# High-part products first and low-part products last in every token-major weight tile of a hybrid decoder block

## The chip, the cores and the metric

The kernel runs on one core of a Trainium2 chip. The metric is the time of one execution on the device in microseconds (us). Its engines are named as the profile names them: PE (TensorE, matrix products), PEld (loading of PE's stationary operand), DVE (VectorE), ACT (ScalarE), POOL (GpSimd) and SP (SyncE, which issues nearly all transfers here).

## The reference

One decoder block on a sequence of 256 tokens, model width 2048, all in float32. A conditioning vector `c` gives a shift, a scale and a gate for each of two halves of the block.

```python
mod = jax.nn.silu(c) @ w_ada[l] + b_ada[l]
sh1, sc1, g1, sh2, sc2, g2 = jnp.split(mod, 6, axis=-1)

h = modulate(rms_norm(x, norm1_g[l]), sh1, sc1)
proj = h @ w_in[l]                                   # 2048 -> 6144: q, k, v, gb, gc, xt
...
attn = moba_attention(q, k, v)...                    # 8 heads of 128; one causal block at 256 tokens
conv = gb * causal_dwconv(gc * xt, conv_w[l], conv_b[l])
mixed = jnp.concatenate([rms_norm(attn, attn_out_g[l]), rms_norm(conv, conv_out_g[l])], axis=-1)
x = x + g1[:, None, :] * (mixed @ w_out[l])          # 2048 -> 2048

h2 = modulate(rms_norm(x, norm2_g[l]), sh2, sc2)
u = causal_dwconv(h2 @ w_ffn_up[l], ffn_conv_w[l], ffn_conv_b[l])    # 2048 -> 11264
u_gate, u_up = jnp.split(u, 2, axis=-1)
ffn = (jax.nn.silu(u_gate) * u_up) @ w_ffn_down[l]   # 5632 -> 2048
x = x + g2[:, None, :] * ffn
```

## The kernel before

**Two parts of every operand.** PE multiplies in a reduced form of float32. To keep accuracy, each operand is split: `hi` is the value rounded to that form, `lo` the remainder. A weight tile W and an activation chunk h then give h_hi W_hi + h_hi W_lo + h_lo W_hi, three products in place of one. In `mm_tok`, `a` is the high part of an activation chunk and `b` its low part; both are stationary operands of 128 x 128 (128 input channels by 128 tokens). The weights are the moving operand, 512 columns wide. The result has the tokens on its partitions ("token-major"), and since there are 256 tokens, each 512 columns of output take two PSUM banks, one for each half of the tokens (index `t`).

**Slots.** The work is a list of slots, one for each weight tile of up to 4 x 128 input channels by 512 columns: 48 for the input projection, 16 for the output projection, 176 for the up projection and 52 for the down projection. The input, output and down projections call `mm_tok`. The up projection has its own loop (L705 and L708), with the weights as the stationary operand, in which the products with `hi` weights and those with `lo` weights already stand in separate runs of 16, in either order by turns. In the first 12 slots of the input projection one slot holds two chunks for each of two projections (for instance v0 and v1), and `mm_tok` runs once for each of them, 12 products each. All other tiles of four chunks are one call of 24 products; some tiles of the down projection have three chunks (18 products) or two (12).

**What a tile passes through.** SP issues the load into a `raw` buffer (5 buffers); ACT copies it to `hi` (L235, 3 buffers); DVE subtracts to get `lo` (L241, 3 buffers) and so frees `raw` for the next load; PE reads `hi` and `lo`. Each engine works through its instructions in the order in which they were emitted. A tile's split is emitted two slots ahead, so its `hi` takes the buffer of the slot before the current one and waits until PE has read that one for the last time.

**What stands around it.** The products with `w_ada` run beside all this, partly on PE (L292), partly on DVE (L296 and L298), from the same `raw` buffers. `evac_in` copies (ACT, L412) or adds (DVE, L414) a finished pair of banks to SBUF; a new output takes two of eight banks in turn. `h_chunks` makes the normalized input chunk by chunk when its shift and scale are known (ACT L762 and L766 for the high part, DVE L769 for the low part). `conv_q` sums squares on DVE (L912), and PE finishes that sum (L916, into `ssC`). `norm2` makes the second norm's factors (L569). In the down projection the stationary chunks come from `up_gate` (high part ACT L641, low part DVE L642). A planner fixed the slot of each of these tasks, and their order within a slot, in the table `CFG`.

**Variants of the order.** In `mm_tok`, `order` runs over chunks `k` and token halves `t`. With `by_t`, the first half's products all come before the second's, so that its bank can be emptied earlier (the last tile of the output projection and the last of each column block of the down projection). With `halved`, the very last tile also splits the second half's 512 columns in two.

Of the kernel before, what the change touches and what calls it, by code (L numbers as in the profile page):

```python
# [110 lines left out]
def tile_block(  # L111
# [6 lines left out]
    mm = nc.tensor.matmul  # L118
# [8 lines left out]
    def bank(name):  # L127
        return ps.tile([P, 512], F32, tag="b", bufs=8, name=name)
# [261 lines left out]
    def mm_tok(key, hi, lo, kts, nk, first, last, by_t=False, halved=False):  # L390

        if first:
            mainp[key] = [bank(f"m{key}{t}") for t in range(2)]
        whole = slice(0, 512)
        order = [(k, t, whole) for t in range(2) for k in range(nk)] if by_t else [(k, t, whole) for k in range(nk) for t in range(2)]
        if halved:
            order = order[:nk] + [(k, 1, slice(h, h + 256)) for h in (0, 256) for k in range(nk)]
        for k, t, s in order:
            o = mainp[key][t][:, s]
            a, b = (v[:, t * P:(t + 1) * P] for v in kts[k])  # L400
            mm(o, a, hi[:, k, s], start=(first and k == 0), stop=False)  # L401
            mm(o, a, lo[:, k, s], start=False, stop=False)  # L402
            mm(o, b, hi[:, k, s], start=False, stop=(last and k == nk - 1 and s.stop == 512))  # L403

    def evac_in(f):
        if in_last.get(f) == now[0]:
# [31 lines left out]
    for i, (fs, k) in enumerate(turns):  # L438
        def near(f, d):
            u = uses[f]  # L440
            n = u.index(i) + d
            return 0 <= n < len(u) and abs(u[n] - i) <= 2

        def go(hi, lo, fs=fs, k=k, new=[not near(f, -1) for f in fs], end=[not near(f, 1) for f in fs]):
            m = 4 // len(fs)
            for h, f in enumerate(fs):
                mm_tok(f, hi[:, h::len(fs)], lo[:, h::len(fs)], [halves(hT[k + j]) for j in range(m)], m, new[h], end[h])

        slots.append((pair_load(k, fs[0]) if len(fs) == 2 else w_load(w_in, k, 4, [(COL[fs[0]] * 512, 512)]), 4, go))
        for f in fs:  # L450
            if not near(f, 1):
                at(len(slots), evac_in, f)
            if i == uses[f][-1]:
                in_last[f] = len(slots)
# [78 lines left out]
    for n, (f, part, k) in enumerate(seq):  # L533
        def go(hi, lo, part=part, f=f, k=k, tf=n == len(seq) - 1):
            mm_tok((part, f), hi, lo, [halves(mixT[k + j]) for j in range(4)], 4, k % 8 == 0, k % 8 == 4, tf)
            if k % 8 == 4:
                done.add((part, f))

        slots.append((w_load(w_out, k, 4, [(f * 512, 512)]), 4, go))
        i = len(slots)  # L540
        if f < 3 and k == 4:
            at(i + CFG["hold"][f], hold_a, f)
        elif f < 3 and k == 12:
            at(i + CFG["evac"][f], evac_out, f)
            at(i + CFG["sq"][f], sq_out, f)
            at(i + CFG["tr"][f], tr_out, f)
        elif f == 3 and k == 4:
            at(i, evac_a, f)
            at(i + CFG["part"], ss_part)
# [124 lines left out]
    SEGS, a = [], 0  # L674
# [5 lines left out]
    for seg, (ga, gb_) in enumerate(SEGS):  # L680
# [43 lines left out]
        for f in range(0, 4, 2):  # L724
            k = ka
# [3 lines left out]
        for f, k, n in parts:  # L729
            def go(hi, lo, seg=seg, f=f, k=k, n=n, ka=ka, kb=kb):  # L730
                last = k + n == kb
                mm_tok(("D", seg, f), hi, lo, [gT[k + j] for j in range(n)], n, k == ka, last,
                       last and seg == len(SEGS) - 1, last and seg == len(SEGS) - 1 and f == 3)

            slots.append((w_load(w_down, k, n, [(f * 512, 512)]), n, go))
            if k + n == kb:
                at(len(slots), evac_down, seg, f)
# [41 lines left out]
    for i, (g, r) in enumerate(fill):  # L779
        if i >= n0 + n1 + n2:  # L780
            extra.setdefault(N_OUT + (i - n0 - n1 - n2) // 2, []).append((g, r))
        if r == g.tiles - 1:
            a = N_OUT + 1 + max(0, (i - n0 - n1 - n2) // 2)
# [212 lines left out]
    for half in range(2):  # L996
        xl, gl = max(in_last[f"x{half}"], in_last[f"c{half}"]), in_last[f"g{half}"]
        o = CFG["conv"][half]
# [101 lines left out]
    for i in range(len(slots)):  # L1100
# [16 lines left out]
        hi, lo = splits.pop(0)  # L1117
# [36 lines left out]
```

## Time and profile before

| | |
|---|---|
| median of 3 runs | 1190.57 us (1190.48 to 1191.34) |
| profiled execution | 1190.94 us, of which the span from the first to the last instruction is 1189.2 us |
| mean granted clock of PE | 0.998 |
| DVE busy | 918.7 us, 77% of the span |
| ACT busy | 615.4 us, 52% |
| loaded from HBM | 310.67 MB, 263 GB/s over the span |
| products at L401, L402 and L403 | 866 each |

The profile records one execution. A row of the order of time gives the start (us from the span's start), the length, engine, line, operation, output and inputs, their shapes, and the count of merged instructions; in brackets stands how long the engine had been idle before it, and what released it. A row of waits gives the waiting instruction, what it waited for, the us in total, how often, and the longest. A row of a stretch gives its bounds, its length, then busy us and instructions of PE, PEld, DVE, ACT and POOL, the granted clock, the DMA engines' busy share and GB/s. Products overlap in the records: a product of 512 columns is shown as 0.39 us, while the next one starts 0.23 us after it.

### The profile page before, as it was taken

Reading aid. Unit: us, or ns where it says so; the run is one execution under the profiler, and the core shown is the slowest. Engines: PE = TensorE matmul, PEld = TensorE weight load, DVE = VectorE, ACT = ScalarE, POOL = GpSimd, SP = SyncE. Lnnn points to the kernel's source line nnn. Section 1 sums busy time; section 2 is a strip of 40 time slices with the busy share of each in tenths; the row PEclk is TensorE's granted clock in tenths of the full one; section 3 lists DMA queues with packets and bytes.
Section 4 is the critical chain, followed back from the end, with each engine's and each line's share of the span. In section 5 each row is a group of like instructions: output and inputs, shape, how many; then the busy total and the mean of one; then the engine's idle time right before and its main releaser. Section 6 shows DMA issues by size and latency. Waiting matters only on the chain.

```text
span 1189.2 us, 15487 instructions
## 1 busy us (share of the span) xinstructions
PE 1162.7 (98%) x6047; PEld 964.5 (81%) x6047; DVE 918.7 (77%) x1106; ACT 615.4 (52%) x854; POOL 1.7 (0%) x9
## 2 busy tenths in 40 slices
PE   5999999999999998999999999999999999999998
PEld 3777788877778777888888888888888888888887
DVE  3889989997889998779888579866755667567676
ACT  5554256456765455556654344654544455344452
POOL 0000000000000000000000000000000000000000
PEclk9999999999999999999999999999999999999999
DMA  9999998999769998664776779754475554664533
GB/s 364 376 400 377 375 372 282 367 353 350 274 232 407 356 370 305 212 211 144 248 283 228 264 273 387 252 190 165 168 233 177 192 190 151 215 227 160 192 127 107
DMA packets 195069, 313.78 MB, mean 264 GB/s; under 512 B 6666, under 2 KB 105772, under 8 KB 194740
## 3 DMA queue, kind: packets, MB, share of 16 engines
q1 hardware_dynamic: 194820, 312.73, 73.6%
q8 instruction: 47, 0.77, 0.3%
q14 instruction: 26, 0.21, 0.1%
q10 hardware_dynamic: 176, 0.07, 0.0%
HBM read 310.67 MB, written 2.10 MB: 263 GB/s over the span
## 4 chain that ended last, share of the span: by engine, by line
PE 90%; DVE 4%; DMA 2%; ACT 2%; issue 1%; SPq 1%; DVEq 0%; ACTq 0%
PE z L705 27%; PE z L708 14%; DMA raw<-in_w_ada_dram 2%; PE ada L292 2%; DVE lo L241 2%; PE mx L401 1%; PE mv L403 1%; PE mx L403 1%; PE mx L402 1%; PE mv L401 1%; PE mv L402 1%; PE mc L401 1%; PE mg L401 1%; PE mc L402 1%; PE mc L403 1%
## 5 line engine op out<-in xcount | busy, mean ns | idle before, releaser
L241 DVE TENSOR_TENSOR lo<-raw,hi 128x2048 fp32r<-128x2048 f32 (+2 forms) x204 | 447.6, 2204 | 146.4 <-ACT hi L235 144.7
L235 ACT ACTIVATE hi<-raw 128x2048 fp32r<-128x2048 f32 (+2 forms) x204 | 375.5, 1849 | 326.4 <-PE z L705 74.4
L705 PE MATMUL z<-h,hi 128*128 128x512 f32 x1408 | 329.2, 390 | 1.9 <-DVE h L594 1.1
L705 PEld LDWEIGHTS z<-h,hi 128*128 128x128 f32 x1408 | 261.3, 188 | 55.6 <-DVE h L594 2.0
L708 PEld LDWEIGHTS z<-h,lo 128*128 128x128 f32 x1408 | 174.9, 192 | 3.4
L708 PE MATMUL z<-h,lo 128*128 128x256 f32 x1408 | 176.3, 283 | 0.0
L298 DVE SCALAR_TENSOR_TENSOR ada<-raw,csil,ada 128x1024 f32<-128x1024 f32 (+2 forms) x165 | 159.5, 968 | 5.5 <-DMA raw<-in_w_ada_dram 1.4
L611 DVE TENSOR_TENSOR ub<-z,ub 128x256 f32<-128x256 f32 x104 | 36.8, 417 | 45.7 <-ACT ub L608 45.6
L625 ACT ACTIVATE uy<-ub,fc,fc 128x256 f32<-128x256 f32 x88 | 45.7, 593 | 5.5 <-DVE uy L632 5.5
L292 PE MATMUL ada<-raw,crep 128*32 128x512 f32 (+1 forms) x320 | 36.4, 567 | 9.9 <-DMA raw<-in_w_ada_dram 9.8
L641 ACT ACTIVATE gh<-uy 128x512 fp32r<-128x512 f32 x22 | 13.9, 632 | 61.2 <-DVE uy L639 61.2
L632 DVE SCALAR_TENSOR_TENSOR uy<-ub,fc,uy 128x254 f32<-128x254 f32 x88 | 42.5, 483 | 3.1
L630 DVE SCALAR_TENSOR_TENSOR uy<-ub,fc,uy 128x255 f32<-128x255 f32 x88 | 42.1, 478 | 1.5 <-ACT uy L625 1.5
L608 ACT ACTIVATE ub<-z 128x256 f32<-128x256 f32 x104 | 31.0, 383 | 22.3 <-PE z L705 22.3
L635 ACT ACTIVATE uy<-uy 128x512 f32<-128x512 f32 x22 | 13.9, 631 | 42.1 <-DVE uy L632 42.1
L292 PEld LDWEIGHTS ada<-raw,crep 128*32 128x32 f32 x320 | 8.5, 114 | 25.9 <-issue 14.5
L642 DVE TENSOR_TENSOR gl<-uy,gh 128x512 fp32r<-128x512 f32 x22 | 15.2, 692 | 15.4 <-ACT gh L641 15.4
L401 PE MATMUL mc<-hi,h 128*128 128x512 f32 x64 | 26.2, 409 | 0.0
L401 PE MATMUL mk<-hi,h 128*128 128x512 f32 x64 | 25.3, 396 | 0.7 <-ACT h L766 0.7
L403 PE MATMUL mv<-hi,h 128*128 128x512 f32 x64 | 25.0, 391 | 0.8 <-DVE h L769 0.8
L401 PE MATMUL mq<-hi,h 128*128 128x512 f32 x64 | 25.4, 397 | 0.4 <-DVE pa_q L414 0.4
L401 PE MATMUL mx<-hi,h 128*128 128x512 f32 x64 | 25.5, 399 | 0.0
(548 smaller groups left out, 1861.4 us busy)
## 6 DMA issues: line engine op xcount, KB each, us to landing
raw<-in_w_ada_dram SPq DMA_DIRECT2D x96, 1024.0 KB
raw<-in_w_ffn_up_dram SPq DMA_DIRECT2D x176, 512.0 KB
raw<-in_w_in_dram SPq DMA_DIRECT2D x48, 1024.0 KB
raw<-in_w_ffn_down_dram SPq DMA_DIRECT2D x24, 1024.0 KB
raw<-in_w_ffn_down_dram SPq DMA_DIRECT2D x24, 768.0 KB
raw<-in_w_out_dram SPq DMA_DIRECT2D x16, 1024.0 KB
xr<-in_x_dram SPq DMA_DIRECT2D x2, 1024.0 KB
x<-in_x_dram SPq DMA_DIRECT2D x8, 256.0 KB
```

Of the source, the lines that this page charges most:

```text
L235: act(hi[:, :nk], t[:, :nk], AF.Copy)
L241: V.tensor_tensor(out=lo[:, :nk], in0=t[:, :nk], in1=hi[:, :nk].bitcast(F32), op=ALU.subtract)
L292: mm(self.acc[q:q + 32, :], crep[:, i, :], t[:, j, :], start=(r == 0 and j < 4), stop=(r == self.tiles - 1 and j >= self.rows - 4), tile_p ...
L298: V.scalar_tensor_tensor(out=self.acc, in0=t[:, j, :], scalar=csil[:, i:i + 1], in1=self.acc, op0=ALU.mult, op1=ALU.add)
L401: mm(o, a, hi[:, k, s], start=(first and k == 0), stop=False)
L403: mm(o, b, hi[:, k, s], start=False, stop=(last and k == nk - 1 and s.stop == 512))
L611: V.tensor_tensor(out=d, in0=zp[grp][ft][:, :256], in1=d, op=ALU.add)
L625: act(y, b, AF.Identity, bias=fcols[3][:, i:i + 1], scale=fcols[2][:, i:i + 1])
L630: V.scalar_tensor_tensor(out=y[:, 1:], in0=b[:, :255], scalar=fcols[1][:, i:i + 1], in1=y[:, 1:], op0=ALU.mult, op1=ALU.add)
L632: V.scalar_tensor_tensor(out=y[:, 2:], in0=b[:, :254], scalar=fcols[0][:, i:i + 1], in1=y[:, 2:], op0=ALU.mult, op1=ALU.add)
L705: mm(zp[grp][ft], hi[:, j, ft * P:(ft + 1) * P], h2T[k + j], start=begins and j == 0, stop=ends and j == 3)
L708: mm(zp[grp][ft][:, :256], lo[:, j, ft * P:(ft + 1) * P], h2T[k + j][:, :256], start=False, stop=False)
```

## The change

Within each call of `mm_tok` the triple a·hi, a·lo, b·hi of one chunk and token half is taken apart. All a·hi and b·hi products come first, in the old order of chunks and halves, and all a·lo products follow in the same order. Where a tile goes token half by token half (`by_t`), or column half by column half (`halved`), this holds within each of these parts, since the sort keeps them apart. The flag that starts an accumulation stays on the first a·hi of a bank; the one that ends it moves to the last a·lo. The number of products, their shapes and their operands are the same, and nothing outside `mm_tok` is touched.

```diff
         if halved:
             order = order[:nk] + [(k, 1, slice(h, h + 256)) for h in (0, 256) for k in range(nk)]
-        for k, t, s in order:
+
+        for low, k, t, s in sorted(((low, *e) for low in (False, True) for e in order),
+                                   key=lambda e: (by_t * e[2], e[3].start * halved * e[2], e[0])):
             o = mainp[key][t][:, s]
             a, b = (v[:, t * P:(t + 1) * P] for v in kts[k])
-            mm(o, a, hi[:, k, s], start=(first and k == 0), stop=False)
-            mm(o, a, lo[:, k, s], start=False, stop=False)
-            mm(o, b, hi[:, k, s], start=False, stop=(last and k == nk - 1 and s.stop == 512))
+            if low:
+                mm(o, a, lo[:, k, s], start=False, stop=(last and k == nk - 1 and s.stop == 512))
+            else:
+                mm(o, a, hi[:, k, s], start=(first and k == 0), stop=False)
+                mm(o, b, hi[:, k, s], start=False, stop=False)
```

## The prediction

> **What bounds the kernel now.** I read the page first (engines, then the chain that ended last), then the waits of the matmul engine, then stretches of the order of time. The engines and the head of the chain:
>
> ```profile
> PE 1162.7 (98%) x6047; PEld 964.5 (81%) x6047; DVE 918.7 (77%) x1106; ACT 615.4 (52%) x854; POOL 1.7 (0%) x9
> ...
> PE 90%; DVE 4%; DMA 2%; ACT 2%; issue 1%; SPq 1%; DVEq 0%; ACTq 0%
> ```
>
> PE is busy for 1162.7 of 1189.2 us and carries 90% of the chain. A change of order that leaves the 6047 products alone can win only from the other 26.5 us, and the list of what PE waited for says where part of those are (us in total, times, longest):
>
> ```profile
> PE ada L292 <- DMA raw<-in_w_ada_dram: 9.8, 3, 6.9
> PE n2b L569 <- DVE n2d L567: 1.5, 1, 1.5
> ...
> PE mv L403 <- DVE h L769: 0.8, 1, 0.8
> PE ssC L916 <- DVE sq L912: 0.7, 1, 0.7
> PE mq L401 <- DVE pa_q L414: 0.4, 1, 0.4
> ```
>
> The reader is to see what is not there: PE never waits for lo L241 or hi L235, the two halves of a weight tile. The obvious gift of the change, more time until the low part is needed, pays nothing, because nobody waits for it. The 9.8 us are loads at the start; n2b and two waits after it, left out here, belong to the norm between output projection and up projection. Three waits (mv, ssC, mq) lie in or beside token-major tiles. Whether those move is the whole question.
>
> **Part 1: the products.** Lines 401 to 403 issue 2598 products (a third on each line), and the change keeps them all, with one weight load each (both counts on the page are 6047). What it alters is which follows which. Neighbouring steps of one tile, its first products and its last, the 24th:
>
> ```profile
> 438.37 0.39 PE L401 MATMUL m('C', 3)0_3728<-hi,mix 128*128 128x512 f32 x1
> 438.60 0.39 PE L402 MATMUL m('C', 3)0_3728<-lo,mix 128*128 128x512 f32 x1
> 438.82 0.39 PE L403 MATMUL m('C', 3)0_3728<-hi,mix 128*128 128x512 f32 x1
> ...
> 443.58 0.39 PE L403 MATMUL m('C', 3)1_3729<-hi,mix 128*128 128x512 f32 x1
> ```
>
> 23 steps in 443.58 - 438.37 = 5.21 us make 0.2265 us a product. From L401 to L402 the stationary operand a stays and the moving one changes; from L402 to L403 the stationary changes: 0.23 and 0.22, so the step does not see it. The chain in order of time has the other pattern, one moving operand under several stationary ones, which the change will use:
>
> ```profile
> 495.00 7.28 PE z L705 x32
> ```
>
> 7.28 / 32 = 0.2275 us. Cost of the new order on PE itself: 0. The two patterns differ by 1 ns a step, and I bound the cost by that either way, 2598 x 0.001 = 2.6 us, a case of its own among the rivals; I take 0 because the first pattern (neighbours with and without a shared operand in one tile) shows none.
>
> A rule speaks against the change here. The Trainium skill, "TensorE: Matmul & The Clock Gate", section "Step-by-step: what each phase is for", says that a stationary operand is loaded apart from the product so that one load can serve many products; the change pulls apart the two that share a. By that rule 866 pairs would lose a saved load each. The trace disagrees that anything is saved: each product has its own load and the step is the same with and without a new operand.
>
> **Part 2: the high part is released earlier.** In a tile of four chunks the last read of hi moves from product 24 to 16, that is 8 x 0.2265 = 1.81 us earlier; with three chunks from 18 to 12 (1.36 us); in the tiles that hold two projections, where each runs its own 12 products, from 24 to 20 (0.91 us). lo's last read moves from 23 to 24, 0.23 us later. The up projection already has tiles in which the high products run first, and shows that the buffer is freed in mid-tile:
>
> ```profile
> 916.01 7.44 PE L705 MATMUL z<-h,hi 128*128 128x512 f32 x32
> 923.29 4.00 PE L708 MATMUL z<-h,lo 128*128 128x256 f32 x32
> ...
> 923.49 1.92 ACT L235 ACTIVATE hi<-raw 128x2048 fp32r<-128x2048 f32 x1 [1.36 <-PE z L705]
> ```
>
> The high products end at 916.01 + 7.44 = 923.45, ACT takes the buffer at 923.49, while the low products go on. So wherever ACT waits for a token-major tile, its hi copy, and behind it in DVE's queue the subtraction for lo, the raw buffer's release and SP's next load, can run up to 1.81 us earlier. All of it is off PE's path, except through what stands behind lo in DVE's queue.
>
> **Part 3: what comes free of this, wait by wait.** First mq, where a new tile's second bank waits until the tile before it is copied out:
>
> ```profile
> 171.27 1.92 ACT L235 ACTIVATE hi<-raw 128x2048 fp32r<-128x2048 f32 x1 [2.41 <-issue]
> 174.24 0.16 DVE L345 TENSOR_TENSOR B<-adaz,vbc 128x4 f32<-128x4 f32 x1 [1.54 <-ACT ada L339]
> ...
> 188.03 1.92 ACT L235 ACTIVATE hi<-raw 128x2048 fp32r<-128x2048 f32 x1 [2.67 <-PE mk L403]
> ...
> 198.48 0.39 PE L403 MATMUL mq<-hi,h 128*128 128x512 f32 x1
> 199.58 0.40 PE L403 MATMUL mq<-hi,h 128*128 128x512 f32 x1
> 200.37 0.51 PE L401 MATMUL mq<-hi,h 128*128 128x512 f32 x1 [0.39 <-DVE pa_q L414]
> ...
> 199.63 1.28 DVE L414 TENSOR_TENSOR pa_q<-mq,pa_q 128x512 f32<-128x512 f32 x2
> ```
>
> The old tile's last product ends at 198.48 + 0.39 = 198.87, but DVE is behind and copies only at 199.63; PE's step is 0.79 where 0.23 is due: 0.56 us lost. DVE has stood without a gap since the h chunks behind 174.24, where it waited 1.54 for ACT, and ACT's hi at 171.27 had waited for the tile that ended then; freed 1.81 us earlier, ACT and DVE run up to 1.5 us ahead, and the next hi (188.03, waiting for mk L403) is freed earlier too. Then DVE copies at about 198.9, one bank takes 0.64, and the bank is needed at 199.58 (third product now, not fourth): under 0.1 us is left. I take -0.5. Ends: -0.56, and +0.23 if DVE is no earlier, since the bank is wanted one product sooner.
>
> Second ssC, the sum of squares of the convolution half:
>
> ```profile
> 346.18 1.91 ACT L235 ACTIVATE hi<-raw 128x2048 fp32r<-128x2048 f32 x1 [0.81 <-PE m('A', 0)1_2919 L403]
> 348.13 2.29 DVE L241 TENSOR_TENSOR lo<-raw,hi 128x2048 fp32r<-128x2048 f32 x1 [1.35 <-ACT hi L235]
> 351.56 0.48 DVE L971 SCALAR_TENSOR_TENSOR cv<-cp,v1c,cv 128x255 f32<-128x255 f32 x1 [0.47 <-ACT cv L970]
> ...
> 378.63 1.80 DVE L912 TENSOR_TENSOR sq<-sq 128x256 f32<-128x256 f32 x4
> ...
> 380.57 0.58 PE L916 MATMUL ssC<-ones,sq 128*128 128x1 f32 x4 [0.70 <-DVE sq L912]
> ```
>
> DVE works from 351.56 (where it had waited for ACT, whose work there stands right behind this hi) to 378.63 + 1.80 = 380.43 with no gap, so its lateness goes back to the hi at 346.18, which waited 0.81 us for a tile's end. Freed 1.81 us earlier, that hi gains the 0.81 that ACT stood idle, and DVE's queue with it, if the loads that it uses on the way are there. 0.81 is more than PE's 0.70: I take -0.7; ends -0.7 and 0.
>
> **Part 4: what is needed earlier.** The product with an activation chunk's low part b moves forward too: for chunk j (from 0) of the first bank from product 6j+3 to 4j+2. Where chunks are made just in time, that costs:
>
> ```profile
> 66.32 0.50 PE L401 MATMUL mv<-hi,h 128*128 128x512 f32 x1
> 66.66 0.40 PE L402 MATMUL mv<-lo,h 128*128 128x512 f32 x1
> 67.90 0.50 PE L403 MATMUL mv<-hi,h 128*128 128x512 f32 x1 [0.84 <-DVE h L769]
> ...
> 67.42 0.75 DVE L769 TENSOR_TENSOR h<-hf,h 128x256 fp32r<-128x256 f32 x2
> ```
>
> Here PE does two products and then waits for the chunk. Now only one stands ahead of the wait, so one more is left behind it: +0.23 us. The chunk itself comes no earlier: the chain before it starts from transposes that PE does at the end of an earlier tile.
>
> At the very first tile the same happens and is free:
>
> ```profile
> 25.55 0.42 DVE L769 TENSOR_TENSOR h<-hf,h 128x256 fp32r<-128x256 f32 x1 [1.18 <-ACT h L766]
> 25.57 0.50 PE L401 MATMUL mk<-hi,h 128*128 128x512 f32 x1 [0.72 <-ACT h L766]
> 33.56 1.54 PE L292 MATMUL ada<-raw,crep 128*32 128x256 f32 x16 [2.22 <-DMA raw<-in_w_ada_dram]
> ```
>
> b is ready at 25.97, wanted at about 25.8: 0.2 us, hidden by the 2.22 us in which PE then waits for a load; without that cover +0.2. In the down projection one chunk is close:
>
> ```profile
> 847.08 1.49 ACT L235 ACTIVATE hi<-raw 128x1536 fp32r<-128x1536 f32 x1 [1.27 <-PE m('D', 1, 0)1_7102 L403]
> 851.73 0.69 DVE L642 TENSOR_TENSOR gl<-uy,gh 128x512 fp32r<-128x512 f32 x1 [0.76 <-ACT gh L641]
> 852.77 0.39 PE L403 MATMUL m('D', 1, 0)0_7101<-hi,gl 128*128 128x512 f32 x1
> ```
>
> gl is ready at 851.73 + 0.69 = 852.42 and used at 852.77, the tile's ninth product; it becomes the sixth, 852.09: 0.33 us too late. But the hi ahead of it in the queues waited 1.27 us for a tile of three chunks, which releases 1.36 us earlier, so gl comes about 1 us earlier as well: 0, and +0.33 if not. Last, the first bank of a tile is complete at product 23 instead of 21, 0.45 us later; the second, which ends the copying, at 24 as before: 0. The last tiles of both projections run bank by bank and keep their end.
>
> **Sum.** +0.23 - 0.5 - 0.7 = -0.97, about -1.0 us: span 1188.2, and the profiled execution (1190.94, its span plus 1.7) 1189.9. That execution lay 0.37 over the median of the three runs, 1190.57; the median becomes 1189.6. Ends: -0.56 - 0.70 = -1.3, or +0.23 + 0.23 + 0.33 + 0.2 = +1.0. About 0.2%, 2.4 us, is what a measurement of this kernel can tell from no change; no end reaches it.
>
> **Rivals.** (1) The gain does not come, the earlier needs stay: slower. Loads are near their limit in the stretch that ends at mq:
>
> ```profile
> 120.00:200.00 80.00, 79.97 (x369) 64.08 (x367) 73.45 (x78) 39.08 (x71) 0.00 (x0) 1.00 0.91 343
> ```
>
> The column before the last is the DMA share, 0.91. If DVE is held by the raw tiles' landing rather than by hi, it runs no earlier, and the price is +0.23 at mv, +0.23 at mq and up to +0.33 at gl and 0.2 at the start: 1191.0 to 1191.6. It decides once DVE gains less than 0.2 us before 199 us. Against it: the waits named at 171.27, 188.03 and 346.18 are on PE or unnamed, not on DMA.
>
> (2) PE's step does depend on the operands' order. Each nanosecond a product is 2.6 us. Upward it takes back the forecast's gain from 0.4 ns and gets past 2.4 us from 1.3 ns; at 2 ns, 5.2 us, the time is 1194.8. Downward, 1 ns gives 1187.0. Against it stand the rows of part 1; for it, that no tile yet has the exact sequence "same bank, same moving, new stationary". The skill's rule above would act through this one.
>
> (3) The slow stretch of PE's clock moves.
>
> ```profile
> 35.03 0.80 PE L401 MATMUL mc<-hi,h 128*128 128x512 f32 x1
> 37.61 0.39 PE L401 MATMUL mc<-hi,h 128*128 128x512 f32 x1
> ```
>
> Six products take 2.58 us where 1.36 is due: 1.2 us lost after the wait at 33.56. If a slightly later end of the first tile spares it, the time is 1188.4; if a second stretch follows, up to 1191.3. The Trainium skill, the same page, Part 1, "What's actually happening", has a gate that halves the clock after an idle window of about 3.4 us; the rows agree with half speed.
>
> **How the numbers follow.** Forecast 0.55 (its own range 1189.2 to 1190.2); rival 1 0.25; rival 2 0.10 (0.06 slower, 0.04 faster); rival 3 0.10, of which 0.02 gets past the 2.4 us. So faster 0.06, slower 0.06, within 0.88. The range takes in the forecast, rival 1 and half of rival 3, 1188.7 to 1191.6, and leaves out about 0.15.
>
> **What would show it.** Right: L401 and L403 of a tile come first with L402 last, steps still 0.2265; ACT's hi released by L403 some 1.8 us before a tile's end; no wait at ssC, under 0.1 us at mq; at mv a wait ahead of the second product, about 0.2 us longer. Wrong: steps off by a nanosecond or more, waits of PE on lo, or new waits of PE for chunks or banks above 1 us in total.

## The result, and the profile after

The changed kernel takes 1189.12 us (median of 17 runs, 1188.79 to 1190.10) where the kernel before takes 1191.23 us (median of 17 runs, 1190.01 to 1193.31): ratio 0.9983, 95% interval 0.9976 to 0.9990, that is 1.2 to 2.9 us less. The time lies in the stated range, 0.5 us under the forecast of 1189.6 and just under the forecast's own range (1189.2 to 1190.2). Against the kernel before on the same chip the gain is 2.1 us, about twice the 1.0 us of the forecast's sum and more than its better end of 1.3. The profiled execution took 1190.10 us with a span of 1188.3 and is the slowest of the 17, so the two profiles differ by only 0.84 us.

The page's rows for the engines and the head of the chain:

```profile
PE 1162.6 (98%) x6047; PEld 964.9 (81%) x6047; DVE 918.2 (77%) x1106; ACT 616.3 (52%) x854; POOL 1.7 (0%) x9
...
PE 92%; DVE 3%; DMA 3%; issue 0%; ACT 0%; SPq 0%; DVEq 0%
```

The work is the same to 0.1 us on PE (1162.7 before). What PE waited for (us in total, times, longest):

```profile
PE n2b L573 <- DVE n2d L571: 1.3, 1, 1.3
PE mv L407 <- DVE h L773: 1.2, 1, 1.2
PE z L709 <- DVE h L598: 1.1, 1, 1.1
PE z L709 <- DVE adaz L334: 0.9, 1, 0.9
...
PE ssC L920 <- DVE sq L916: 0.4, 1, 0.4
```

mq is gone from the list, ssC fell from 0.7 to 0.4, n2b from 1.5 to 1.3, mv rose from 0.8 to 1.2; the two waits of the up projection stay. In the changed kernel L406 is a·hi, L407 b·hi and L404 a·lo. The mv tile, the stretch where mq used to wait (with DVE's copy there, which is now the one that waits), and the tile before ssC in the order of time:

```profile
66.40 0.49 PE L406 MATMUL mv<-hi,h 128*128 128x512 f32 x1
68.11 0.50 PE L407 MATMUL mv<-hi,h 128*128 128x512 f32 x1 [1.22 <-DVE h L773]
...
199.52 0.47 PE L406 MATMUL mq<-hi,h 128*128 128x512 f32 x1
199.83 0.40 PE L407 MATMUL mq<-hi,h 128*128 128x512 f32 x1
200.07 0.39 PE L406 MATMUL mq<-hi,h 128*128 128x512 f32 x1
...
199.17 1.29 DVE L418 TENSOR_TENSOR pa_q<-mq,pa_q 128x512 f32<-128x512 f32 x2 [0.36 <-PE mq L404]
...
375.73 0.39 PE L406 MATMUL m('C', 1)0_3252<-hi,mix 128*128 128x512 f32 x1
377.31 0.39 PE L407 MATMUL m('C', 1)1_3253<-hi,mix 128*128 128x512 f32 x1
377.54 0.39 PE L404 MATMUL m('C', 1)0_3252<-lo,mix 128*128 128x512 f32 x1
379.13 0.39 PE L404 MATMUL m('C', 1)1_3253<-lo,mix 128*128 128x512 f32 x1
379.93 0.58 PE L920 MATMUL ssC<-ones,sq 128*128 128x1 f32 x4 [0.41 <-DVE sq L916]
```

The steps are 0.226 us among the high products (1.58 / 7 from 375.73) and 0.227 among the low ones (1.59 / 7 from 377.54), as before. ACT takes the buffer while the low products run:

```profile
358.84 1.92 ACT L235 ACTIVATE hi<-raw 128x2048 fp32r<-128x2048 f32 x1 [1.76 <-DMA raw<-in_w_out_dram]
360.79 2.29 DVE L241 TENSOR_TENSOR lo<-raw,hi 128x2048 fp32r<-128x2048 f32 x1 [1.50 <-ACT hi L235]
...
377.74 1.92 ACT L235 ACTIVATE hi<-raw 128x2048 fp32r<-128x2048 f32 x1 [1.70 <-PE m('C', 1)1_3253 L407]
```

The last high product ends at 377.31 + 0.39 = 377.70 and ACT starts at 377.74; the tile's last product ends 1.8 us later. The first two rows are the limit of that: there ACT waits not for PE but for a load, and DVE stands idle for 1.50 us behind it.

### The profile page after: what moved, and what is told of

Read it like the earlier page. It is cut to its first block, busy times and chain, and to the rows that moved or that the text cites. A ratio compares the mean times of both kernels' runs of the same rounds, so it can differ in the third digit from the quotient of the medians.

```text
span 1188.3 us, 15497 instructions
## 1 busy us (share of the span) xinstructions
PE 1162.6 (98%) x6047; PEld 964.9 (81%) x6047; DVE 918.2 (77%) x1106; ACT 616.3 (52%) x854; POOL 1.7 (0%) x9
## 4 chain that ended last, share of the span: by engine, by line
PE 92%; DVE 3%; DMA 3%; issue 0%; ACT 0%; SPq 0%; DVEq 0%
PE z L709 27%; PE z L712 14%; DMA raw<-in_w_ada_dram 3%; PE ada L292 2%; PE mc L406 1%; PE mc L407 1%; PE mg L406 1%; PE mc L404 1%; PE mg L407 1%; PE mg L404 1%; PE mx L406 1%; DVE lo L241 1%; PE mx L407 1%; PE mx L404 1%; DVE ada L298 1%; PE mv L407 1%
## 5 line engine op out<-in xcount | busy, mean ns | idle before, releaser
L406 PE MATMUL mc<-hi,h 128*128 128x512 f32 x64 | 26.5, 414 | 0.0
L407 PE MATMUL mv<-hi,h 128*128 128x512 f32 x64 | 25.1, 392 | 1.2 <-DVE h L773 1.2
L406 PE MATMUL mk<-hi,h 128*128 128x512 f32 x64 | 25.3, 396 | 0.7 <-ACT h L770 0.7
L407 PE MATMUL mc<-hi,h 128*128 128x512 f32 x64 | 25.9, 405 | 0.0
L406 PE MATMUL mx<-hi,h 128*128 128x512 f32 x64 | 25.5, 399 | 0.0
```

The costliest lines, as they stand in the source:

```text
L407: mm(o, b, hi[:, k, s], start=False, stop=False)
```

## The experiments

My theory was that the gain comes from the early release of `hi`, which lets ACT and DVE run ahead. The rivals were the late need of `lo`, the order of operands on PE itself, and the slow stretch of PE's clock near 35 us. All kernels issue the products from one rewritten loop (`n` is 0 for a·hi, 1 for b·hi, 2 for a·lo), which puts them on one line; the diffs show only the order.

A table helps to read them: starts of products in each kernel's profile, in us. "First" is the first product of tile 0, "mv" the stretch from the start of tile 6 (the mv tile) to that of tile 7, "mq" the 28 steps from the start of tile 28, "28 to end" all from there to the end of the last product.

| kernel | first | mv | mq | 28 to end |
|---|---|---|---|---|
| before | 25.57 | 7.78 | 7.14 | 985.48 |
| old_again | 27.53 | 8.74 | 7.13 | 985.93 |
| after | 25.80 | 8.19 | 6.48 | 984.14 |
| new_again | 25.36 | 8.01 | 6.50 | 984.03 |
| late_hi | 25.48 | 8.03 | 7.34 | 987.84 |
| mid_only | 25.41 | 7.79 | 6.47 | 984.87 |
| rest_only | 27.18 | 8.53 | 7.37 | 984.87 |
| a_b_lo | 27.83 | 7.33 | 6.66 | 984.52 |
| pairs_b_last | 27.69 | 7.56 | 6.49 | 984.15 |
| old_pairs | 27.08 | 10.48 | 6.48 | 983.90 |
| mv_b_last | 27.51 | 6.67 | 6.48 | 984.21 |
| mv_b_last_old | 27.74 | 7.54 | 6.48 | 984.33 |
| mv_b_last_fill | 25.30 | 6.67 | 6.48 | 983.97 |

From the start of tile 12 to that of tile 28 every profile takes 93.06 to 93.08 us, whatever the order of the 384 products in between. What differs stands ahead of tile 12 and behind tile 28.

**Both orders once more.** old_again is the old order from the common loop, new_again the new one.

> The kernel before, its products issued from the rewritten loop that all experiments share: ratio 1.000, and a second profile of the old order. It shows how far the old order's stalls vary from execution to execution. If the waits that the change removed (mq 0.56 us of PE's steps, ssC 0.86) and the slow stretch of PE's clock near 35 us (1.2 us lost) are fixed parts of the kernel, this profile repeats them within 0.1 us; if the 1.2 us by which the medians differ more than the two profiles comes from stalls that vary, they differ here by some tenths.

> The changed kernel from the same rewritten loop: ratio 0.9983 as measured, within 0.0007, and a second profile of the new order. The first one was of the slowest of its runs (1190.1 where the median is 1189.1). If a slow stretch of the clock made that run slow, this profile, when it is a faster run, has a shorter or no stretch near 35 us; if not, the difference lies in PE's waits behind it.

old_again: 1190.87 us, ratio 1.000 (0.9991 to 1.0009). new_again: 1189.03 us, ratio 0.9988 (0.9979 to 0.9997), where the kernel before took 1190.83 us. The waits behind tile 28 repeat; what varies is the start, and with it mv. Waits of the old order's second profile, and the same 16 products at the start in the first and the second old profile:

```profile
PE mv L414 <- DVE h L781: 1.8, 1, 1.8
...
PE ssC L928 <- DVE sq L924: 0.7, 1, 0.7
PE mq L414 <- DVE pa_q L426: 0.4, 1, 0.4
PE at L858 <- DVE pa_k L847: 0.3, 1, 0.3
```

```profile
19.35 1.07 PE L292 MATMUL ada<-raw,crep 128*32 128x256 f32 x16
```

```profile
20.38 1.94 PE L292 MATMUL ada<-raw,crep 128*32 128x256 f32 x16
```

In old_again PE is still slow at 20 us: 1.94 us for what took 1.07. Its first tile starts 2 us later; the second tile starts no later (34.3 against 35.0 us), since the first profile waits 2.22 us for a load between the two tiles and the second does not; but at mv the old order then waits 1.8 us in place of 0.8. The 13 profiles fall into six early starts (25.3 to 25.8 us) and seven late ones (27.1 to 27.8). The slow stretch at 35 us (a granted clock of 0.50 from 34.2 to 37.3 us in the first old profile, 1.00 in the second) stands in both profiles of the main comparison and in mid_only, but not in old_again or new_again.

**One product held back.** Edit, on top of the new order:

```diff
+        seq.append(seq.pop(max(i for i, e in enumerate(seq) if e[0] == 1)))   # last b*hi behind all a*lo
```

> The new order with one product moved: in each call the last product with the weights' high part comes after all products with the low part. hi is then held to the tile's end as before the change, while the low part is still needed late and the products are still grouped. Early release of hi is the cause (my theory): ACT's hi waits for the tile's end again, the waits at mq (0.56 us) and ssC (0.3 us more) come back, the longer wait at mv stays; time 1190.9 to 1191.6, ratio 0.9995 to 1.0004. The late need of lo is the cause (rival): all stays as in the changed kernel, ratio 0.998. The order of operands on PE is the cause (rival): also 0.998, with steps unlike 0.2265 us.

1192.00 us, ratio 1.0012 (1.0004 to 1.0021), on the same chip on which the new order had 0.9988 (0.9979 to 0.9997). Waits:

```profile
PE ssC L928 <- DVE sq L924: 0.7, 1, 0.7
PE mq L414 <- DVE pa_q L426: 0.6, 1, 0.6
PE at L858 <- DVE pa_k L847: 0.5, 2, 0.3
...
PE m('D', 1, 0)0_7101 L414 <- DVE gl L654: 0.2, 1, 0.2
```

One product in each call makes 3.0 us between the medians. `lo` is needed as late as in the changed kernel, and the products are grouped as there, so neither is the cause: the early release is. From tile 28 to the end its profile is 3.8 us longer than new_again's: 0.9 at mq, 1.4 from there to 288 us, where the two waits at L858 stand, 0.4 at ssC, 0.5 at the tile that waits for gl, and smaller ones. It came out slower than expected because the earlier needs of the new order now bite without their cover; mq (0.6 in place of 0.4) and gl show that.

**Where it is won.** mid_only has the new order in tiles 12 to 27 only, rest_only from tile 28 on only, the old order elsewhere.

```diff
+        mode = "new" if 12 <= now[0] < 28 else "old"    # mid_only
+        mode = "new" if now[0] >= 28 else "old"         # rest_only
```

> The new order only in the tiles 12 to 27, the ones of the input projection that stand before the wait at mq; old order everywhere else. My theory (early release of hi lets ACT and DVE run ahead): the mq wait goes and with it 0.65 us between the first product of tile 28 and the fifth of tile 29 (7.1 us in the two old profiles, 6.5 in the two new ones); ssC keeps its 0.7 us wait and n2b its 1.5. Ratio 0.9994. If the gain belongs to the order of products as such and grows with the number of products in it (rival), 384 of 2598 products would bring 15% of 2 us, 0.3 us, and the mq wait would not be special.

> The complement behind it: the new order only from tile 28 on, old order before. My theory: the mq wait stays at 0.4 us (steps 7.1 us), the stretch from tile 28 to the end gains the rest, 1.0 to 1.3 us (a wait at L858 for pa_k that one old profile has and no new one, ssC 0.3 to 0.4, n2b 0.15): ratio 0.9990. With mid_only the two should add up to the changed kernel's gain behind tile 27, 1.6 us. If the gain is all at mq (rival), this one is 1.000.

mid_only: 1190.40 us, ratio 0.9999 (0.9991 to 1.0008). rest_only: 1189.75 us, 0.9993 (0.9984 to 1.0002). Neither interval excludes 1, so the times leave the split open; the profiles do not. Of mid_only and then of rest_only:

```profile
PE n2b L582 <- DVE n2d L580: 1.5, 1, 1.5
...
PE ssC L929 <- DVE sq L925: 0.7, 1, 0.7
```

```profile
PE n2b L582 <- DVE n2d L580: 1.3, 1, 1.3
...
PE mq L415 <- DVE pa_q L427: 0.6, 1, 0.6
...
PE ssC L929 <- ACT hi L235: 0.2, 1, 0.2
```

With the new order ahead of it only, mq is gone (7.1 to 6.47 us) and ssC and n2b are as before. With it behind only, mq waits 0.6 (one product sooner, as the prediction's other end had it), and ssC and n2b fall. From tile 28 to the end each gains 0.8 us on the mean of the two old profiles (985.7 - 984.87); together that is 1.6, the new order's gain there (985.7 - 984.1). The two old profiles differ by 0.45, so this addition is no finer than that.

**What is still lost at mv.** a_b_lo orders each call as a·hi, b·hi, a·lo in three groups; pairs_b_last has a·hi, a·lo, b·hi in the first 12 tiles; old_pairs has the old order there. `rank` gives the place of a·hi, b·hi and a·lo; the new order has (0, 0, 1).

```diff
+        mode = "a_b_lo"                                                          # a_b_lo, all tiles
+        mode = "a_lo_b" if now[0] < 12 else "new"                                # pairs_b_last
+        mode = "old" if now[0] < 12 else "new"                                   # old_pairs
...
+            rank = dict(new=(0, 0, 1), late=(0, 0, 1), a_b_lo=(0, 1, 2), a_lo_b=(0, 2, 1))[mode]
```

> Three groups in each call: all products a*hi, then all b*hi, then all a*lo. hi is released at the same product as in the new order; only the need of the activation's low part b moves later, from product 2 to product 5 in the two-projection tiles and to product 9 in the others. My theory of the costs: the mv wait shrinks by three steps, 0.7 us (from 1.1 to 1.2 idle to 0.4 to 0.5), all gains stay: 0.5 to 0.7 us faster than the changed kernel, ratio 0.998 beside its 0.9985. If the chunk's high part is what comes late (rival), the wait only moves to a*hi and the time stays.

> The changed kernel, but in the first 12 tiles the products with the activation's low part come last (a*hi, a*lo, b*hi), so hi is held to the end there and b is needed only at product 9 of a call. If the wait at mv is only a matter of when b is needed, it goes (1.1 us idle, 1.5 us of steps), and the time is 1.0 to 1.5 us under the changed kernel, ratio 0.9975. If early release in the first 12 tiles matters (rival), DVE is later and some of it comes back as waits between 60 and 110 us; old_pairs, which held hi there too, lost nothing by that.

> The new order only from the 13th tile on; the first 12 tiles, of two projections each, keep the old one. My theory: the mv tile waits as before the change (step of 1.24 us ahead of the third product in place of 1.71 ahead of the second), 0.2 to 0.5 us, and mq and ssC keep the gain: 0.2 to 0.5 us faster than the changed kernel, ratio 0.9979. If the early release in the first 12 tiles is what sets DVE ahead at mq (rival), the 0.56 us wait there comes back and nothing is won: 0.9983 to 0.9988.

a_b_lo: 1188.99 us, 0.9991 (0.9982 to 1.0000). pairs_b_last: 1187.74 us, 0.9980 (0.9971 to 0.9989). old_pairs: 1188.77 us, 0.9988 (0.9980 to 0.9997) beside new_again's 0.9988, so the old order in these tiles neither won nor lost as far as this can tell. The mv rows of a_b_lo, pairs_b_last and old_pairs:

```profile
PE mv L415 <- DVE h L782: 0.4, 1, 0.4
```

```profile
PE mv L415 <- DVE h L782: 0.6, 1, 0.6
...
PE mc L415 <- ACT pa_k L425: 0.3, 1, 0.3
```

```profile
PE mv L414 <- DVE h L781: 1.9, 1, 1.9
```

a_b_lo did what was expected at mv (0.4) but not in the time: its 28 to end is 0.4 to 0.5 us longer than the new order's, of which 0.2 at mq; why is open. In pairs_b_last 0.6 us stay, although b is wanted only at product 9, and a bank comes late (pa_k). All three are late starts. old_pairs waits 1.9 with b at product 3; six products later, 1.36 us, that leaves 0.5, which is what pairs_b_last has. With hi released early, a_b_lo waits 0.4 at product 5, which for the changed kernel's product 2 would mean 0.4 + 3 x 0.23 = 1.1 (an estimate; no profile has a late start with b at product 2).

What the chunk's low part waits for is DVE's queue. In the first old profile ACT has the high parts ready at 64.04 us, and DVE makes the low parts only at 67.42, behind four `w_ada` products. Those products in old_again and in a_b_lo, both late starts:

```profile
64.55 3.11 DVE L298 SCALAR_TENSOR_TENSOR ada<-raw,csil,ada 128x512 f32<-128x512 f32 x4 [0.47 <-DMA raw<-in_w_ada_dram]
```

```profile
63.57 3.11 DVE L298 SCALAR_TENSOR_TENSOR ada<-raw,csil,ada 128x512 f32<-128x512 f32 x4
```

In the five late starts that hold `hi` to the tile's end in the tiles ahead (old_again, rest_only, old_pairs, pairs_b_last and, below, mv_b_last_old), DVE first waits 0.45 to 0.47 us for a load there. In the two late starts with the early release (a_b_lo and, below, mv_b_last) and in all six early starts it does not. That fits a `raw` buffer that comes free sooner and so brings its load forward; this link is argued, not tested.

**The version that the experiments point to.** The new order everywhere, with b·hi last in the mv tile alone; beside it the old order in the other 11 tiles of two projections, and eight products run twice in the load wait of the first tile.

```diff
+        mode = "a_lo_b" if now[0] == 6 else "new"                                # mv_b_last
+        mode = "a_lo_b" if now[0] == 6 else "old" if now[0] < 12 else "new"      # mv_b_last_old
+        if 8 and key == "k1" and now[0] == 0:                                    # mv_b_last_fill
+            for i, (n, k, t, s) in enumerate(seq[:8]):
...
```

> The changed kernel, with the activation's low part last (a*hi, a*lo, b*hi) in the one tile at mv only, the seventh. b is needed there at product 9 of the call in place of product 2, 1.6 us later, against a wait of 1.1 to 1.2 us idle: if that wait is the whole remaining cost of the change, it goes, the 24 products and the loads behind them take 6.5 to 7.0 us from this tile to the next in place of 8.0 to 8.2, and the time is 1.0 to 1.4 us under the changed kernel: ratio 0.9975, like pairs_b_last or a little better, since that one lost 0.4 us between tiles 7 and 12 on late banks. Rival: ACT or DVE fall behind by what hi is held longer and give it back by tile 12; then it is 0.998 to 0.9985.

> The same, with the old order in the other 11 tiles of two projections. If the early release in those tiles brings the chunk at mv earlier (old profiles wait 0.8 to 1.9 us there, new ones 1.1 to 1.2 although one product sooner), this one waits 0.5 us longer at mv when the start is late, and is up to 0.5 us slower than mv_b_last; if it brings nothing, they are equal.

> mv_b_last with 8 products more: the first 8 of the second call in the first tile are run twice (the second run starts the sum anew), which fills 1.8 us of the 2.2 to 2.5 us in which PE then waits for a load. If the idle stretch brings on the slow clock near 35 us (rival 3), its slow stretch is gone; where the start is early this costs nothing, where it is late (first product at 27.5 us) it costs up to 1.8 us less what PE would have waited. Median: 0 to 0.3 us better if the slow stretch is in one execution of four, as in the profiles so far; 1 us or more better only if nearly all timed runs have it; up to 1.5 us worse if late starts are common.

mv_b_last: 1187.64 us, ratio 0.9970 (0.9959 to 0.9982), the lowest of all medians. mv_b_last_old: 1188.30 us, 0.9975 (0.9965 to 0.9984). mv_b_last_fill: 1187.65 us, 0.9973 (0.9963 to 0.9984). The three intervals overlap, so what sets the versions apart is read from the profiles. The mv tile's b·hi in mv_b_last and in mv_b_last_old, both late starts:

```profile
67.31 1.98 PE L415 MATMUL mv<-hi,h 128*128 128x512 f32 x8
```

```profile
67.73 1.45 PE L415 MATMUL mv<-hi,h 128*128 128x512 f32 x5 [0.54 <-DVE h L782]
```

The wait is gone in the first (6.67 us from mv to the next tile) and 0.54 us long in the second, where `hi` is held in the tiles ahead: in these two profiles the early release there brings the chunk at least 0.5 us sooner, counted from the tile's start. The eight extra products cost nothing and bring nothing in the median: either the slow stretch does not set that median, or filling the wait does not take it out. Which of the two stays open, since neither this profile nor mv_b_last's has one.

## Why the prediction was right, and where a term was off

**Products on PE: right.** Steps of 0.226 to 0.227 us, and 93.06 to 93.08 us for tiles 12 to 27 in every order; no lost weight load shows. Rival 2 is out, and with it the saved load that it rested on.

**Early release: right, and shown** by late_hi, which takes it away and leaves the rest, and by the two halves, mid_only and rest_only.

**mq: right.** -0.5 was forecast, -0.65 measured (7.13 to 6.48). DVE now waits 0.36 us for PE there.

**ssC: too large.** -0.7 was forecast, 0.3 came in the first profile (a wait of 0.41 in place of 0.70). The condition that the prediction named, loads that are there in time, failed. DVE ran further ahead than the 0.81 that was expected: what it began at 351.56 before, it begins at 349.50. But ACT's hi at 358.84 waited 1.76 us for its load, and DVE, idle for 1.50 behind it, starts the next `lo` only 0.5 us earlier than before (361.26 to 360.79). Rival 1's mechanism holds at that place. The prediction's "no gap" from 351.56 on overlooked a wait of 0.27 us for ACT at 358.68, without harm to the reading.

**mv: right for an early start only.** +0.23 was forecast; early starts show +0.2 to +0.4 (7.78 and 7.79 to 8.01 and 8.19). "The chunk itself comes no earlier" is wrong for a late start, where old profiles take 8.5 to 8.7 us and the new order, by the estimate above, about 8.0. The prediction followed the chunk back to transposes on PE and left out the last link, DVE's queue with the `w_ada` products and their load.

**n2b and the attention's transposes: missed.** The sum had 0 for n2b, which fell by 0.15 to 0.2. The wait for pa_k at L858 (0.3 in old_again, 0.5 in late_hi, none in a profile of the new order from tile 28 on) was not in the first profile and could not be read there.

**gl, first tile, last bank: right.** No wait for gl in the changed kernel; without its cover, in late_hi, it is there. The first tile lost 0.23 us (its second product waits 0.46 us after the first) and the load wait took it.

**The sum.** Behind tile 28 the forecast had -1.2 and the profiles have -1.6 on the mean (-1.3 for the two of the main comparison); ahead of it +0.23 against something between +0.4 and -0.7 by the start. If half of the starts are late, as 7 of the 13 are, that makes about -1.7 on the mean, an estimate that is near the 1.8 us between new_again and its kernel before and under the 2.1 of the main comparison. Two small gains that were set to 0 or not seen, and a cost that is one only half of the time, are most of the difference from -1.0. That the time came so near to 1189.6 is in part luck: the forecast started from 1190.57, a median of 3 runs, where 17 runs have 1191.23, and this 0.66 made up for over half of the gain that was missing. And the 2.4 us that the prediction took for the least change that can be told was too much: with 17 runs each the interval is 0.8 us to either side.

**Rival 3: open.** The slow stretch stands in both profiles of the main comparison, so it does not make the difference between those. Early starts take 40.6 to 40.8 us from the first product to the mv tile with it and 39.7 to 40.0 without. How often it comes is not on record, but a mean granted clock of 0.998 or less stands beside 30 of the 83 timed runs of the kernel before that were made with the experiments, and beside 1 of the 28 of the new order. This mean does not say where the slow time lay (the changed kernel's profile has the stretch at 0.999), so it is a hint and no more: part of the 1.8 to 2.1 us between the medians may be slow stretches that became rarer, and no run here tests that.

## What to carry to other kernels

When buffers are few, the order of reads within a tile decides when a buffer comes free, and moving its last reader forward by a third of a tile can be worth more than the slack given to the other operand: here nobody waited for the late part, and the gains that the profiles show came from the release. The same reordering brings some other operand's first read forward, so list those reads and put them back where an operand is made just in time; here one tile of 292 was worth 1.3 to 1.5 us in the profiles (8.01 and 8.19 to 6.67 at mv), and the medians agree, with less certainty since they are from two chips (1189.03 and 1187.64). Before a term under 1 us is trusted, compare two profiles of the same kernel: half a microsecond of this one depended on how its start fell.

## What the runs showed of the hardware

The step from product to product was 0.226 to 0.227 us whether the stationary operand changes with every product (new order) or with two of three (old order).

PE's slow time at the start does not last equally long: the same 16 products took 1.07 us at 19.35 in one execution and 1.94 us at 20.38 in another of the same order, and first tiles begin at 25.3 to 25.8 or at 27.1 to 27.8 us. Later slow stretches come and go too: from 34.2 to 37.3 us the granted clock was 0.50 in one old profile and 1.00 in the other. In old_pairs one fell behind the mv wait (0.50 from 69.6 to 72.7 us), and that tile took 10.5 us where other old-order profiles have 7.8 to 8.7. So two single profiles of this kernel can differ by more than the change is worth.
